# A one-core decoder layer: memory tokens fetched together ahead of the first step of dilated values, and the values' stores issued from the ACT queue

## The chip, the cores and the metric

The kernel runs on one core of a Trainium2 chip. The metric is the device time of one execution in microseconds (us); the time of a kernel is the median of several runs. The core has five engines that each work through their own list of instructions in order: TensorE (PE in the profile) multiplies matrices and transposes, VectorE (DVE) and ScalarE (ACT) do elementwise work, GpSimd (POOL) a little of it, and SyncE (SP) does nothing here but issue transfers (DMAs) between device memory and on-chip memory. Instructions of different engines are ordered only by semaphores: an instruction that waits holds everything behind it on its own engine.

## The reference

One layer on 512 tokens of width 1024, all in float32. Around every part stand a norm before and a norm after, with a gain each:

```
h = x + 0.5 * post(SwiGLU_1(pre(x)))
u = pre(h)
proj = u @ w_in                      # recurrence q,f,i,gate | dilated q,k,v x3 | memory queries | branch gates
y_hg  = gated linear recurrence (HGRN2) on chunks of 64 tokens, 4 heads of 128
y_dil = sliding-window attention at dilations 1, 4, 16, merged over the three
y_mem = softmax(mq @ mk.T) @ mv,   mk, mv = split(rmsnorm(mem, mem_norm_w) @ w_mem_kv)
y = sum over branches of sigmoid(gate_b) * (y_b @ w_br_b)
h = h + post(y @ w_out)
h = h + 0.5 * post(SwiGLU_2(pre(h)))
```

`mem` holds 256 memory tokens of width 1024. They are normed, transposed and projected to keys and values; this does not depend on the 512 tokens.

## The kernel before

Matrices are kept with the contracted index on the 128 partitions. Every float32 operand of a big product is split into two parts: a rounded one, hi, that ACT writes, and the rest, lo, that DVE writes (`split`, L160). A product is three matmuls (hi·hi, hi·lo, lo·hi), L333 to L335 for 512 columns and L353 to L355 for 256. Pairs of weight columns go through a scheme of seven half-size products in place of eight (`pair`, L358); their sums of weights are made by DVE (`total`) or by an adding transfer that POOL issues (L302).

The mixing part (`mixing`, L900) runs a list of steps, `ORDER` (L42). Those that matter here: "hg0" and "hg1" project two heads of the recurrence each (three `pair` calls: f, q and the output gate), "v1", "v2" and "v0" project the values of one dilation for all four heads, "prep" norms and transposes the memory tokens, and "kv" projects them.

- A values step (`values`, L837) loads a 1024x512 block of weights in four pieces of 512 KB, splits it, and makes four blocks of 24 matmuls, one for each 128 tokens. ACT copies each block out of PSUM (L850), and `put_values` (L853) stores it to device memory, from where the attention later reads it in another order of rows.
- The step "prep" starts `mem_prep` (L523), a Python generator. For each of two tiles of 128 tokens it fetches two halves of 256 KB (L530), squares them on ACT (L174, the sum of squares comes along), raises the sum to the power -1/2 on POOL (L181), scales by it and the gain on DVE (L190) and transposes on PE, two groups of four (L344). ACT and DVE split what the transposes give into the tiles `mT`.

The order of all work comes from a small planner in Python. Each matmul that is written advances a clock (`tick`, L109). A generator that yields a number of microseconds is picked up again that much later (`LAT`, L47), and what it then writes lands between the matmuls of the main steps. So the engines' lists are fixed in advance; a matmul or transpose whose operand is late holds the PE list behind it. All fetches are issued on SP. Those made by `fetch` (L139) stand in the SP list in the order written; weight loads (`bring`, L145) may move up but keep their mutual order. A transfer on SP waits for its target's buffer to be free, and also for the transfer eight places earlier in the rotation of eight completion semaphores. Buffers: 4 stages of 512 KB for weights, 18 split weights, 37 slots of 128x512, 5 weight sums, and 3 PSUM banks (`px`) for all side work.

Names in the lists of instructions: `st`, `sh` are staged weights, `sum` a weight sum, `w` a split weight, `s` a slot, `v` the values in device memory, `ps` and `px` PSUM banks of the main steps and of side work, `ident` the identity matrix of a transpose.

Of the kernel before, what the change touches and what calls it, by code (L numbers as in the profile page):

```python
# [17 lines left out]
P = 128  # L18
# [20 lines left out]
NST = 4  # L39
HT = T // 2  # L40

ORDER = ("hg0", "v1", "prep", "hg1", "v2", "kv", "v0", "dil0", "mq0", "mq1", "dil1", "b_hg", "b_mem", "b_dil")  # L42

CHUNKS1 = (2, 4, 4, 4, 4, 4)
CHUNKS2 = (2, 4, 4, 4, 4, 4)

LAT = dict(comb=1.0, mem0=0.5, mem1=8.0, mem2=1.5, hg=1.5, hgx=6.0, hg1=6.0, hg2=11.0, hg3=6.0, hg4=6.0, dil0=4.0, dil1=17.0, dil2=5.0,  # L47
           dil3=3.0, norm=8.0, mnorm=5.0, start=0.1, step=2.0, keep=2.0)
PLAN = dict(early1=2, plain1=2, early2=2, plain2=2)
HALVES = (slice(0, 512), slice(512, 1024))  # L50


class Layer:
# [469 lines left out]
    def mem_prep(self, mem, w, mT):  # L523

        gain = self.bcast_gain(w)
        for t in range(2):
            ts = slice(t * P, (t + 1) * P)
            m = [self.slot() for _ in range(2)]
            for hf in range(2):
                self.fetch(m[hf], mem[ts, HALVES[hf]])  # L530
            hf = 0
            for x in self.normed(m, gain, LAT['mnorm'], self.paux):
                if isinstance(x, float):
                    yield x
                    continue
                for i in range(2):
                    hi, lo = mT[2 * hf + i]
                    self.split(hi[:, :, ts], lo[:, :, ts], x[:, 2 * i:2 * i + 2, :])
                hf += 1
# [313 lines left out]
    def put_values(self, v, name):  # L853

        d = self.dram.tile([T, 512], F32, tag=name, name=name)
        for t in range(NT):
            self.nc.sync.dma_start(out=d[t * P:(t + 1) * P, :], in_=v[t][:, 0, :])
        return d

    def get_values(self, d, g, hp):  # L860
# [39 lines left out]
    def mixing(self, a, ready, nbias):  # L900
# [41 lines left out]
        z, vd = None, {}  # L942
        for n, step in enumerate(ORDER):
            if step in ("hg0", "hg1"):
# [18 lines left out]
            else:  # L963
                b, y, tasks, w = {"b_hg": (0, y_hg, t_hg, "w_br_hg"), "b_mem": (2, y_mem, t_mem, "w_br_mem"), "b_dil": (1, y_dil, t_dil, "w_br_dil")}[step]
                self.need(*tasks)
                z = self.branch(b, y, w_in, a[w][0], z, n == len(ORDER) - 1)
        return z
# [140 lines left out]
```

## Time and profile before

| what | value |
| --- | --- |
| time, median of 3 runs | 1394.15 us (1392.47 to 1395.41) |
| the profiled execution's own time | 1396.16 us |
| its span in the trace | 1394.4 us |
| mean granted clock of TensorE | 0.988 of full speed |
| busy: PE, DVE, ACT, POOL | 1341.6, 1016.6, 744.5, 161.8 us (96, 73, 53, 12% of the span) |
| DMA: share of the 16 engines on SP's queue, on POOL's | 41.6%, 16.4% |

The profile lists one execution. PE is busy in nearly all of it, so what counts is where PE stands still, which instruction it stood before, and whether its clock was lowered after it. The clock column gives the granted clock as a share of 2.4 GHz: 1.00 is full speed and 0.50 is 1.2 GHz. Busy times of the other engines are averages over stages; only in the stretch around a PE wait do they say something about the time.

The steps of interest in the trace: "v1" runs its 96 matmuls from 428 to 450.6 us, "hg1" follows until 504 us, then "v2".

### The profile page before, as it was taken

What the parts mean: (1) busy time and instruction counts of PE and PEld (TensorE: products, weight loads), DVE (VectorE), ACT (ScalarE), POOL (GpSimd) and SP (SyncE); (2) the same over time, 40 slices, a digit from 0 to 9 for tenths busy, and PEclk for the clock granted to TensorE, in tenths of its full rate; (3) what the DMA queues carried; (4) which work ended last, traced back from release to release, by engine and by line L of the source; (5) the groups of instructions that cost most, each with busy time, mean ns of one, the idle gap of its engine ahead of it and who ended that gap; (6) DMA issues with size and microseconds to landing.
All of it is one profiled execution on the core that took longest, in us unless ns stands there. A gap on an engine that the chain in (4) does not pass through costs nothing.

```text
span 1394.4 us, 24579 instructions
## 1 busy us (share of the span) xinstructions
PE 1341.6 (96%) x9197; PEld 1242.3 (89%) x9197; DVE 1016.6 (73%) x1932; ACT 744.5 (53%) x1527; POOL 161.8 (12%) x204
## 2 busy tenths in 40 slices
PE   6999999999999699998899999999999999999997
PEld 6999999999788688898889899999889999999995
DVE  6887777776888574576777787787569777767765
ACT  6675545554576464353655555555457655445541
POOL 1011110110200100111201201110010100100000
PEclk9999999999999899999899999999999999999998
DMA  9676565656536534576456656665365776655513
GB/s 269 141 185 180 137 151 148 158 143 179 175 96 178 150 106 136 148 184 150 103 126 149 166 127 160 154 163 131 111 219 145 175 181 160 150 145 140 149 46 136
DMA packets 264238, 210.95 MB, mean 151 GB/s; under 512 B 10645, under 2 KB 216886, under 8 KB 264118
## 3 DMA queue, kind: packets, MB, share of 16 engines
q1 hardware_dynamic: 242870, 171.56, 41.6%
q0 software_dynamic: 21248, 37.82, 16.4%
q8 instruction: 72, 1.18, 0.4%
q14 instruction: 48, 0.39, 0.1%
HBM read 162.12 MB, written 9.47 MB: 123 GB/s over the span
## 4 chain that ended last, share of the span: by engine, by line
PE 46%; DVE 3%; issue 2%; DMA 2%; ACT 0%; POOL 0%; DVEq 0%; POOLq 0%; ACTq 0%
PE ps L354 9%; PE ps L355 9%; PE ps L353 9%; PE ps L334 3%; PE ps L333 3%; PE ps L335 3%; PE px L340 2%; PE px L333 2%; PE px L334 2%; PE px L335 2%; DVE s L158 1%; DVE w L158 1%; PE px L344 1%; DMA sh<-in_w_in_dram 1%; DMA sum<-sh 1%
## 5 line engine op out<-in xcount | busy, mean ns | idle before, releaser
L161 ACT ACTIVATE w<-sum 128x512 fp32r<-128x512 f32 x288 | 180.1, 631 | 222.1 <-PE ps L354 174.9
L158 DVE TENSOR_TENSOR w<-sum,w 128x512 fp32r<-128x512 f32 x288 | 196.6, 689 | 87.1 <-ACT w L161 85.5
L353 PE MATMUL ps<-xhi,w 128*128 128x256 f32 x864 | 247.4, 286 | 0.9 <-ACT s L371 0.9
L355 PE MATMUL ps<-xhi,w 128*128 128x256 f32 x864 | 246.0, 285 | 0.7 <-DVE w L158 0.7
L354 PE MATMUL ps<-xlo,w 128*128 128x256 f32 x864 | 245.5, 284 | 0.0
L161 ACT ACTIVATE w<-st 128x512 fp32r<-128x512 f32 x260 | 163.5, 630 | 137.4 <-PE ps L354 97.1
L158 DVE TENSOR_TENSOR w<-st,w 128x512 fp32r<-128x512 f32 x260 | 177.3, 689 | 34.0 <-ACT w L161 32.1
L158 DVE TENSOR_TENSOR s<-s,s 128x256 f32<-128x256 f32 (+3 forms) x316 | 177.2, 566 | 19.0 <-ACT s L161 4.2
L353 PEld LDWEIGHTS ps<-xhi,w 128*128 128x128 f32 x864 | 166.7, 193 | 3.5 <-ACT s L371 1.1
L354 PEld LDWEIGHTS ps<-xlo,w 128*128 128x128 f32 x864 | 166.5, 193 | 2.5 <-issue 0.2
L355 PEld LDWEIGHTS ps<-xhi,w 128*128 128x128 f32 x864 | 166.8, 193 | 0.9 <-DVE w L158 0.9
L302 POOL DMA_DIRECT2D sum<-st x72 | 62.7, 871 | 642.9 <-DVE s L158 374.9
L158 DVE TENSOR_TENSOR sum<-sum,st 128x512 f32<-128x512 f32 x144 | 99.3, 690 | 46.0 <-issue 34.9
L158 DVE TENSOR_TENSOR s<-s,ps 128x256 f32<-128x256 f32 (+1 forms) x194 | 92.5, 478 | 33.5 <-PE ps L335 25.0
L333 PE MATMUL px<-s,s 128*128 128x512 f32 x288 | 112.6, 391 | 0.0
L334 PE MATMUL px<-s,s 128*128 128x512 f32 x288 | 112.5, 391 | 0.0
L335 PE MATMUL px<-s,s 128*128 128x512 f32 x288 | 112.0, 389 | 0.0
L302 POOL DMA_DIRECT2D sum<-sh x72 | 63.6, 883 | 301.2 <-DMA sh<-in_w_in_dram 101.5
L353 PE MATMUL ps<-t3hi,w 128*128 128x256 f32 x288 | 83.3, 289 | 0.5 <-DVE s L158 0.5
L353 PE MATMUL ps<-t4hi,w 128*128 128x256 f32 x288 | 82.0, 285 | 0.8 <-ACT s L374 0.8
L354 PE MATMUL ps<-t3lo,w 128*128 128x256 f32 x288 | 82.5, 286 | 0.0
L353 PE MATMUL ps<-t2hi,w 128*128 128x256 f32 x288 | 82.4, 286 | 0.0
(185 smaller groups left out, 3433.4 us busy)
## 6 DMA issues: line engine op xcount, KB each, us to landing
st<-in_ffn_w_gu_dram SPq DMA_DIRECT2D x48, 512.0 KB, 4.8
st<-in_w_in_dram SPq DMA_DIRECT2D x48, 512.0 KB, 4.2
st<-in_ffn_w_down_dram SPq DMA_DIRECT2D x44, 512.0 KB, 3.9
sum<-in_ffn_w_gu_dram SPq DMA_DIRECT2D x80, 256.0 KB, 3.3
sum<-sh POOLq DMA_DIRECT2D x72, 256.0 KB, 3.8
sum<-st POOLq DMA_DIRECT2D x72, 256.0 KB, 3.8
sum<-in_w_in_dram SPq DMA_DIRECT2D x64, 256.0 KB, 3.2
sh<-in_ffn_w_gu_dram SPq DMA_DIRECT2D x40, 256.0 KB, 3.5
```

What stands on the lines that cost most here:

```text
L158: self.pin(self.nc.vector.tensor_tensor(out=out, in0=a, in1=b, op=op))
L161: self.pin(self.nc.scalar.activation(hi, src, AF.Copy))
L302: self.nc.gpsimd.dma_start(out=u, in_=x, accum_op=ALU.add)
L333: mm(out, lhsT=lhs[0], rhs=rhs[0], start=first, stop=False)
L334: mm(out, lhsT=lhs[0], rhs=rhs[1], start=False, stop=False)
L335: mm(out, lhsT=lhs[1], rhs=rhs[0], start=False, stop=last)
L340: self.nc.tensor.matmul(out, lhsT=lhsT, rhs=rhs, start=start, stop=stop, **k)
L344: self.nc.tensor.transpose(out, in_, self.ident)
L353: mm(out, lhsT=lh, rhs=rh, start=first and k == 0, stop=False, skip_group_check=True)
L354: mm(out, lhsT=lh, rhs=rl, start=False, stop=False, skip_group_check=True)
L355: mm(out, lhsT=ll, rhs=rh, start=False, stop=k == 3, skip_group_check=True)
```

## The change

Three edits. The list of steps has "prep" ahead of "v1" and no longer behind it. `mem_prep` fetches both tiles of memory tokens (four halves) at once, directly behind the two halves of the gain, and then yields a new latency `mload` of 10 us before the first norm; before, it fetched a tile when its turn came. And `put_values` issues its stores from the ACT queue (`nc.scalar`) where it was SP's (`nc.sync`).

```diff
-ORDER = ("hg0", "v1", "prep", "hg1", "v2", "kv", "v0", "dil0", "mq0", "mq1", "dil1", "b_hg", "b_mem", "b_dil")
+ORDER = ("hg0", "prep", "v1", "hg1", "v2", "kv", "v0", "dil0", "mq0", "mq1", "dil1", "b_hg", "b_mem", "b_dil")
...
-           dil3=3.0, norm=8.0, mnorm=5.0, start=0.1, step=2.0, keep=2.0)
+           dil3=3.0, norm=8.0, mnorm=5.0, mload=10.0, start=0.1, step=2.0, keep=2.0)
...
         gain = self.bcast_gain(w)
+        ms = [[self.slot() for _ in range(2)] for _ in range(2)]
+        for t in range(2):
+            for hf in range(2):
+                self.fetch(ms[t][hf], mem[t * P:(t + 1) * P, HALVES[hf]])
+        yield LAT['mload']
         for t in range(2):
             ts = slice(t * P, (t + 1) * P)
-            m = [self.slot() for _ in range(2)]
-            for hf in range(2):
-                self.fetch(m[hf], mem[ts, HALVES[hf]])
             hf = 0
-            for x in self.normed(m, gain, LAT['mnorm'], self.paux):
+            for x in self.normed(ms[t], gain, LAT['mnorm'], self.paux):
...
-            self.nc.sync.dma_start(out=d[t * P:(t + 1) * P, :], in_=v[t][:, 0, :])
+            self.nc.scalar.dma_start(out=d[t * P:(t + 1) * P, :], in_=v[t][:, 0, :])
```

What this makes of the engines' lists, first on SP, before, from the last weight piece that is loaded during "v1" on (`st_6030`; `v_5451` are the values of "v1", `s_5464` a half of the gain, `s_5468` and `s_5613` halves of the two tiles of memory tokens):

```order
L151 DMA st_6030<-in_w_in_dram 128x2x512
L857 DMA v_5451<-s_5332 128x512
...
L151 DMA sum_5730<-in_w_in_dram 128x4x128
...
L151 DMA st_6040<-in_w_in_dram 128x2x512
L857 DMA v_5451<-s_5449 128x512
L141 DMA s_5464<-in_mem_norm_w_dram 128x512
...
L141 DMA s_5468<-in_mem_dram 128x512
...
L151 DMA sh_5728<-in_w_in_dram 128x4x128
L151 DMA st_6050<-in_w_in_dram 128x2x512
L151 DMA sh_6816<-in_w_in_dram 128x4x128
L151 DMA sum_6818<-in_w_in_dram 128x4x128
L141 DMA s_5613<-in_mem_dram 128x512
```

And now, from the same weight piece on (it is called `st_6051`):

```order
L151 DMA st_6051<-in_w_in_dram 128x2x512
L141 DMA s_5265<-in_mem_norm_w_dram 128x512
L141 DMA s_5266<-in_mem_norm_w_dram 128x512
L141 DMA s_5269<-in_mem_dram 128x512
L141 DMA s_5270<-in_mem_dram 128x512
L141 DMA s_5271<-in_mem_dram 128x512
L141 DMA s_5272<-in_mem_dram 128x512
L151 DMA sum_5730<-in_w_in_dram 128x4x128
L151 DMA sum_5733<-in_w_in_dram 128x4x128
L151 DMA st_6061<-in_w_in_dram 128x2x512
L151 DMA sh_5728<-in_w_in_dram 128x4x128
```

The six loads have moved ahead of the next weight sums, the four stores of "v1" have left the list, and no weight load stands between the two tiles of memory tokens.

On PE, before, the transposes of the first tile (`px_5595`, `px_5604`) stand in "hg1", behind the first product of its second pair (`ps_5736`):

```order
L335 MATMUL ps_5420<-w_5293,xlo_91 128x512
L353 MATMUL ps_5506<-xhi_88,w_5509 128x256
...
L340 MATMUL px_5582<-s_5364,s_5360 128x128 x4
L344 MATMUL px_5588<-ident,s_5361 128x128 x4
...
L355 MATMUL ps_5736<-xhi_88,w_5740 128x256
L344 MATMUL px_5595<-ident,s_5482 128x128 x4
...
L344 MATMUL px_5604<-ident,s_5484 128x128 x4
```

Now they stand in "v1", ahead of its fourth block (`ps_5486`), and those of the second tile (`px_5512`, `px_5521`) in the third product of the first pair of "hg1":

```order
L335 MATMUL ps_5411<-w_5313,xlo_91 128x512
L344 MATMUL px_5452<-ident,s_5405 128x128 x4
L344 MATMUL px_5461<-ident,s_5407 128x128 x4
L333 MATMUL ps_5486<-w_5279,xhi_88 128x512
...
L354 MATMUL ps_5617<-t1lo,w_5618 128x256
L344 MATMUL px_5512<-ident,s_5480 128x128 x4
L355 MATMUL ps_5617<-t1hi,w_5619 128x256
L353 MATMUL ps_5617<-t1hi,w_5618 128x256
L344 MATMUL px_5521<-ident,s_5482 128x128 x4
L340 MATMUL px_5603<-s_5384,s_5380 128x128 x4
```

Between the two groups for the second tile and the end of "v1" there are 12 + 12 + 8 matmuls of 256 columns. Four matmuls of the recurrence of "hg0" (L340) come right behind.

On DVE, before, the elementwise work of the recurrence of "hg0" (the last four of it here) is followed at once by the lo parts of the weights of "hg1":

```order
L158 TENSOR_TENSOR s_5388<-s_5388,s_5111 128x512
L158 TENSOR_TENSOR s_5389<-s_5389,s_5111 128x512
L158 TENSOR_TENSOR s_5384<-s_5384,s_5321 128x512
L158 TENSOR_TENSOR s_5385<-s_5385,s_5321 128x512
L158 TENSOR_TENSOR w_5532<-sum_5528,w_5531 128x512
L158 TENSOR_TENSOR w_5550<-sum_5490,w_5549 128x512
```

Now the scaling of the first tile (`v_5401` and the two L190) stands amid it:

```order
L158 TENSOR_TENSOR s_5381<-s_5381,s_5328 128x512
L180 TENSOR_SCALAR v_5401<-ss_1119_5395,ss_1121_5398 128x1
L190 SCALAR_TENSOR_TENSOR s_5405<-s_5269,r_5402,s_5265 128x512
L190 SCALAR_TENSOR_TENSOR s_5407<-s_5270,r_5402,s_5266 128x512
L158 TENSOR_TENSOR s_5418<-s_5369 128x512
...
L158 TENSOR_TENSOR s_5419<-s_5419,s_5341 128x512
L158 TENSOR_TENSOR s_5258<-px_5452,s_5257 128x2x128
L158 TENSOR_TENSOR w_5586<-sum_5582,w_5585 128x512
...
L180 TENSOR_SCALAR v_5476<-ss_1136_5470,ss_1138_5473 128x1
L158 TENSOR_TENSOR w_5705<-sh_5542,w_5704 128x512
L190 SCALAR_TENSOR_TENSOR s_5480<-s_5271,r_5477,s_5265 128x512
```

Six instructions of the recurrence now come behind the scaling of the first tile, and then, up to that of the second, eight weight instructions of 512 columns and four lo parts of the transposed tokens of 256.

## Rows read from the trace of the kernel before

**Rows 1.** Waits of PE, whole span: what waited for whom, total us, times, longest.

```profile
PE px L344 <- DVE s L190: 22.4, 8, 9.1
```

**Rows 2.** Timeline of PE around v1 and hg1, and one row near 1036: start, us, instruction, idle before.

```profile
445.17 0.39 PE L333 MATMUL ps<-w,xhi 128*128 128x512 f32 x1
...
450.61 0.28 PE L353 MATMUL ps<-xhi,w 128*128 128x256 f32 x1
...
452.04 0.28 PE L353 MATMUL ps<-t2hi,w 128*128 128x256 f32 x1
...
466.02 1.09 PE L344 MATMUL px<-ident,s 128*128 128x128 f32 x4 [6.74 <-DVE s L190]
...
478.44 0.63 PE L344 MATMUL px<-ident,s 128*128 128x128 f32 x4 [3.06 <-DVE s L190]
481.07 1.09 PE L344 MATMUL px<-ident,s 128*128 128x128 f32 x4 [2.00 <-DVE s L158]
...
1035.85 0.38 PE L334 MATMUL ps<-xlo,w 128*128 128x256 f32 x1 [1.94 <-DVE xlo L158]
```

**Rows 3.** Windows: length, busy PE, PEld, DVE, ACT, POOL, clock, DMA, GB/s.

```profile
466.00:468.90 2.90, 2.88 (x14) 2.90 (x15) 2.90 (x7) 0.38 (x1) 0.00 (x0) 0.51 0.17 30
...
481.00:486.00 5.00, 4.93 (x24) 4.96 (x25) 3.32 (x10) 3.11 (x6) 0.00 (x0) 0.51 0.00 0
...
435.00:438.00 3.00, 3.00 (x15) 2.49 (x14) 1.99 (x6) 2.97 (x5) 0.00 (x0) 1.00 1.13 306
438.00:441.00 3.00, 3.00 (x15) 2.49 (x14) 3.00 (x4) 2.60 (x6) 0.00 (x0) 1.00 0.33 126
440.00:455.00 15.00, 15.00 (x85) 13.17 (x84) 14.48 (x24) 11.71 (x24) 0.65 (x1) 1.00 0.36 116
560.00:580.00 20.00, 20.00 (x107) 16.59 (x106) 7.41 (x15) 3.66 (x7) 1.78 (x2) 1.00 0.58 156
1033.00:1036.00 3.00, 1.06 (x6) 0.67 (x5) 2.56 (x5) 2.34 (x7) 0.75 (x1) 1.00 0.61 232
```

**Rows 4.** Timeline of SP's queue, 432 to 500 us: start, us, transfers issued.

```profile
433.67 0.37 SPq L151 DMA_DIRECT2D st<-in_w_in_dram  x1
438.81 8.85 SPq L857 DMA_DIRECT2D v<-s  x3
...
454.01 0.93 SPq L141 DMA_DIRECT2D s<-in_mem_dram  x2
...
469.79 2.65 SPq L141 DMA_DIRECT2D s<-in_mem_dram  x2
```

**Rows 5.** Waits of SP's queue, whole span.

```profile
SPq L857 <- ACT s L850: 52.9, 11, 8.7
```

**Rows 6.** Timeline of ACT, 432 to 500 us.

```profile
442.43 0.62 ACT L640 ACTIVATE s<-s 128x512 f32<-128x512 f32 x1
...
460.63 0.63 ACT L174 ACTIVATE s<-s 128x512 f32<-128x512 f32 x1 [4.94 <-DMA s<-in_mem_dram]
...
461.92 0.63 ACT L174 ACTIVATE s<-s 128x512 f32<-128x512 f32 x1 [0.57 <-DMA s<-in_mem_dram]
...
475.90 0.61 ACT L174 ACTIVATE s<-s 128x512 f32<-128x512 f32 x1
```

**Rows 7.** Timeline of DVE, 445 to 495 us.

```profile
445.32 2.50 DVE L158 TENSOR_TENSOR s<-s,s 128x512 f32<-128x512 f32 x4
...
470.65 0.76 DVE L158 TENSOR_TENSOR s<-px,s 128x256 fp32r<-128x256 f32 x2 [1.29 <-ACT s L161]
...
477.54 1.42 DVE L190 SCALAR_TENSOR_TENSOR s<-s,r,s 128x512 f32<-128x512 f32 x2 [0.69 <-POOL r L181]
```

**Rows 8.** DMA issues of the page: KB each, median us from issue to landing.

```profile
v<-s SPq DMA_DIRECT2D x12, 256.0 KB, 2.0
```

## Prediction, on record before the changed kernel ran

> **What bounds the kernel now.** I read four views, in this order: the page's busy times with the clock, the waits of PE, the timeline of PE where these waits lie, and the timelines of SP, ACT and DVE in the same stretch. PE is the bound: it is busy nearly throughout, so a change can gain only where PE stands still or runs at a lowered clock. The waits of PE show one large entry, transposes (L344) that wait for the scaled tile from DVE's L190 [rows 1]. The rest of that entry lies at the start of the kernel and at the other norms, which the change does not touch. In the timeline the reader is to see three stops of PE inside "hg1", each in front of a transpose: 6.74, 3.06 and 2.00 us, in all 11.8 us [rows 2]. They are the transposes of the memory tokens. After the stops the granted clock is 0.51, so PE runs at 1.2 instead of 2.4 GHz: 2.88 us of work in 466.0 to 468.9 and 4.93 us in 481.0 to 486.0 [rows 3]. This is 7.81 us of work that would take half as long, so another 3.9 us. Together the memory tokens cost 11.8 + 3.9 = 15.7 us.
>
> Why the tokens are late stands in the timeline of SP. After the weight load at 433.67 the queue holds the stores of the values, and each of these waits on SP for ACT's copy: the three stores begin at 438.81 and take 8.85 us until all are issued [rows 4]. Over the whole span SP waited 52.9 us for such copies [rows 5]. The first tile of tokens is issued only at 454.01, and ACT's squares wait for it until 460.63 and 461.92 [rows 4, 6]. The second tile stands behind a weight load whose buffer is still in use and goes out at 469.79.
>
> **The loads, earlier.** In the new SP list the six loads come right behind the weight load of 433.67. That is issued by 434.04; a pair takes 0.93 us [rows 4], so the gain goes out until 434.97, the first tile until 435.90, the second until 436.83. Their targets have been free long before by the order of the list. From issue to use the two halves of the first tile took 460.63 - 454.01 = 6.6 and, issued half a pair later, 461.92 - 454.48 = 7.4 us [rows 4, 6]. Taken over, the halves are there at 441.6 and 442.9. This is an estimate with two ends: it can be sooner, which gains nothing (next paragraph), and it can be later, since the DMA engines are full until about 439 (share 1.13, then 0.33 [rows 3]) and the loads add 6 x 256 KB = 1.5 MB. At the 306 GB/s of that row this takes 4.9 us, so everything has landed by 444, and by 445 with one us for completion. I take the measured 7.4 us.
>
> **First stop that is left (S1).** PE reaches the first transposes behind three blocks of "v1", at 445.17, where the fourth block starts now [rows 2]. ACT gets to the squares behind the exponentials of "hg0", whose last one before that point starts at 442.43 and takes 0.62 us [rows 6]; with one store issued by ACT itself, for which I take SP's 0.37 us for a load [rows 4], that is 443.4. The second square starts some 0.6 us later, at 444.0. From the start of the second square to the transpose it took 478.44 - 475.90 = 2.54 us [rows 2, 6], through DVE, POOL and DVE again. So PE goes on at 446.5: S1 = 1.4 us. Bounds: with no issue cost 1.0; with the second half landing at 445 it is 445 + 2.54 - 445.17 = 2.4; with the landing 1.5 us later still, 4.
>
> **Second stop that is left (S2).** The tile's scaling stands in DVE's list amid the recurrence of "hg0", and DVE is busy 14.48 of 15 us there [rows 3], so what comes behind is pushed back. The scaling starts 0.9 us ahead of the transpose (477.54 against 478.44 [rows 2, 7]), at 445.6, and its two instructions take 1.42 us: 447.1. Then come six instructions of the recurrence at 2.50 / 4 = 0.63 us, 3.8 us; eight weight instructions, 5.0 us; four lo parts at 0.76 / 2 = 0.38 us, 1.5 us [rows 7]. That is 457.4. POOL's power, whose operand is made one instruction before the end of this list, adds about 0.3 us, and the scaling again 0.9 us to the transpose: 458.6. PE gets there by 446.5 + 0.9 (two groups of transposes) + 5.44 (a block, 445.17 to 450.61) + 32 matmuls at 1.43 / 12 = 0.12 us, 3.8 us [rows 2], at 456.7. So S2 = 1.9 us. Bounds: 0, if DVE gains 2 us by finding its operands ready, and 4, if ACT's splits, which alternate with DVE's here, come late by as much.
>
> **Clock.** A stop of 1.94 us near 1036 left the granted clock at 1.00 [rows 2, 3]; the stop of 3.06 us was followed by the lower clock. S1 and S2 lie nearer to the first. I take no loss, and 3.9 / 2 = 2 us for each stop as the other end.
>
> **What lies beside other work.** The stores no longer hold up SP, but the loads behind them feed splits that PE did not wait for here, so this alone gains nothing. On ACT the twelve stores cost at most 12 x 0.37 = 4.4 us; eight of them lie in "v2" and "v0", where ACT is as little busy as 3.66 of 20 us and PE fully [rows 3]. A store waits there only for ACT's own copy and for a transfer issued long before. The four of "v1" have their price in S1 and S2. With PE 12 us earlier, the weights of the next pairs are wanted earlier: counting on through both lists with the same durations, DVE has the first summed weight of the second pair of "hg1" at about 465, and PE wants it at about 469 (estimates).
>
> The Trainium skill speaks against the second part of the change. "DMA: Bandwidth & Descriptors", section "Issuing engines are not separate DMA queues", says that transfers issued by different engines run on the same 16 DMA engines and interleave, and that issuing from several engines saves only the sequencer's time. By it the first store of "v1", no longer behind the loads but beside them, can put off the tokens by its 256 KB, 0.9 us at 306 GB/s, S1 would be 2.3 and the time 0.9 us longer. The rows agree in that the engines are full just there (1.13 [rows 3]); they do not show two queues side by side at this place, and the store is issued only near 439, when the loads are mostly under way.
>
> **Sum.** 15.7 - 1.4 - 1.9 = 12.4 us less. The profiled execution took 1396.16 us (span 1394.4), so its counterpart would take 1383.8 us (span 1382.0). The median of the runs is 1394.15, 2.0 us below the profiled one; the prediction for the median is 1394.15 - 12.4 = 1381.8 us. Runs of this kernel differ by some 3 us, so I call 0.2% (2.8 us) the least that can be told from no change.
>
> **Rivals.**
> - Both stops vanish, because DVE keeps up: the whole 15.7 us, 1378.5. For it: PE is the bound elsewhere at the same mix of work. Against it: ACT is not free for the squares before 443.
> - The tokens stay late: the DMA engines are full when the loads are issued, S1 and S2 become 4 us each and each is followed by the lower clock, 2 us each. That is 12 of 15.7 us, so 1390.4. For it: the DMA share of 1.13; against it: only 1.5 MB stand in front or beside.
> - DVE becomes the bound. The scaling and lo parts of two tiles, 2 x (1.42 + 4 x 0.38 + 0.2) = 6.3 us, used to fall into PE's stops and are now added where DVE has 0.5 us free in 15. If PE has to wait for all of them beyond S1 and S2, 15.7 - 3.3 - 6.3 = 6.1 us are left: 1388.
> - Slower: ACT is held by its own stores. If an issue on ACT blocks it until the transfer has landed, the first two stores of "v1", one ahead of the squares and one ahead of the weight splits, put off everything behind them. The median landing is 2.0 us [rows 8], under load up to 7.4 as above: 2 x 7.4 = 14.8 us on the path, the lower clock twice 4 us, S1 and S2 3.3 us, against 15.7 us: 1394.15 + 6.4 = 1400.5. It decides from (15.7 - 3.3 - 4) / 2 = 4.2 us a store. Against it: on SP three stores and their waits went out in 8.85 us, and the next load followed, so an issue does not hold its queue until landing.
> - The change does not do what it says: the loads stay behind something on SP (a buffer, or one of the eight semaphores). The transposes then wait as before, 1394. Against it: the transfers that the loads wait for by rotation all stand ahead of the weight load of 433.67 in the list.
>
> **How the numbers follow.** Chances: the forecast 0.52, both stops gone 0.12, late tokens 0.15, DVE bound 0.12, slower by ACT 0.05, no effect 0.04. The forecast's own range is S1 + S2 from 1 to 5.7, so 1379.5 to 1384.2. The range of 8 in 10 takes in both stops gone and reaches over the DVE case to late tokens: 1378 to 1390.5. Faster by over 0.2%: 0.52 + 0.12 + 0.12 + 0.12 of the late tokens = 0.88. Within 0.2%: 0.04 and 0.03 of the late tokens, 0.07. Slower: 0.05.
>
> **What would show it.** In the profile after: SP issues the tokens at about 435 to 437, not 454 and 470. PE has a stop of 1 to 2.4 us before the first transposes near 445 and one of about 2 us near 457, none of 6.74 us, and "v2" begins some 12 us earlier. The clock stays at 1.00 from 440 to 500. Wrong would be: squares that still wait for the tokens beyond 445, the clock at 0.5 in "v1" or "hg1", stops of PE in front of weights (L353 to L355) after 460, or idle time of ACT right behind its stores.

## The result, and the profile after

The kernel after takes 1377.81 us (median of 4 runs, 1376.86 to 1380.12), the kernel before 1394.78 us beside it: a ratio of 0.9879, 95% interval 0.9858 to 0.9900, which is 17.0 us less. Predicted were 1381.8 us and a range from 1378.0 to 1390.5. So the direction and the place were right, and the fall was larger than the whole range allowed, by 0.2 us. The profiled execution of after has a span of 1375.1 us.

PE's waits, its stops in v1 and hg1, and the clock (length, busy PE, PEld, DVE, ACT, POOL, clock, DMA, GB/s) in the profile after; they answer to [rows 1 to 3]:

```profile
PE px L344 <- DVE s L190: 15.9, 7, 10.4
```

```profile
445.76 1.29 PE L344 MATMUL px<-ident,s 128*128 128x128 f32 x8 [1.22 <-DVE s L190]
...
457.80 0.63 PE L344 MATMUL px<-ident,s 128*128 128x128 f32 x4 [1.44 <-DVE s L190]
```

```profile
440.00:500.00 60.00, 57.31 (x418) 51.96 (x417) 48.65 (x97) 39.71 (x83) 7.13 (x9) 1.00 0.54 151
```

Three stops of together 11.8 us have become two, S1 = 1.22 and S2 = 1.44 us, and the clock is at full speed (2.4 GHz) in all of these 60 us, where before two stretches ran at half. SP's queue and ACT's timeline in the same place [rows 4 and 6], and the scalings on DVE [rows 7]:

```profile
434.98 2.00 SPq L141 DMA_DIRECT2D s<-in_mem_dram  x4
...
452.60 1.33 SPq L151 DMA_DIRECT2D sum<-in_w_in_dram  x2
```

```profile
435.53 1.28 ACT L623 ACT_TABLE_LOAD   x1
436.18 0.35 ACTq L859 DMA_DIRECT2D v<-s  x1
...
442.61 0.62 ACT L174 ACTIVATE s<-s 128x512 f32<-128x512 f32 x1
...
443.23 0.62 ACT L174 ACTIVATE s<-s 128x512 f32<-128x512 f32 x1
```

```profile
444.87 1.41 DVE L190 SCALAR_TENSOR_TENSOR s<-s,r,s 128x512 f32<-128x512 f32 x2 [0.68 <-POOL r L181]
...
456.90 1.41 DVE L190 SCALAR_TENSOR_TENSOR s<-s,r,s 128x512 f32<-128x512 f32 x2 [0.44 <-POOL r L181]
```

All four halves of the tokens are issued by 437 us. The squares have no wait in brackets: the tokens were there. The issue of a store at 436.18 lies inside the table load of 435.53 to 436.81, so ACT lost nothing by it. Behind the next store, of 444.43, ACT stands still for 2.5 us, but what it waits for there is an operand from DVE, whose list now has the scaling ahead of it. The page's line for these stores, against [rows 8]:

```profile
v<-s ACTq DMA_DIRECT2D x12, 256.0 KB, 2.6
```

Behind hg1, however, PE kept gaining. Since executions start up to 3 us apart, the table compares stretches, worked out from PE's timeline: "v1 to v0" runs from the first matmul of L333 in v1 to the first of L353 behind v0, "dil0 to dil1" from there to the next L333 behind dil1. The last column goes from the stop of some 5 us at the start of the memory queries (664 us before, 651 after) to the next one (683 and 668 us). The experiments below are in it. The rows between which the stretches of the first profiles lie, first before, then after, each with the recurrence's matmuls that stand near the end of "hg1":

```profile
427.96 0.40 PE L333 MATMUL ps<-w,xhi 128*128 128x512 f32 x1
...
504.08 0.40 PE L333 MATMUL ps<-w,xhi 128*128 128x512 f32 x1
...
505.22 1.06 PE L340 MATMUL px<-s,s 128*128 128x128 f32 x8
...
588.85 0.28 PE L353 MATMUL ps<-xhi,w 128*128 128x256 f32 x1
...
797.47 0.40 PE L333 MATMUL ps<-s,w 128*128 128x512 f32 x1
```

```profile
428.00 0.40 PE L333 MATMUL ps<-w,xhi 128*128 128x512 f32 x1
...
490.89 1.06 PE L340 MATMUL px<-s,s 128*128 128x128 f32 x8
...
492.58 0.40 PE L333 MATMUL ps<-w,xhi 128*128 128x512 f32 x1
...
575.55 0.28 PE L353 MATMUL ps<-xhi,w 128*128 128x256 f32 x1
...
778.56 0.40 PE L333 MATMUL ps<-s,w 128*128 128x512 f32 x1
```

| profile | v1 to v0 | of it v1, hg1 | dil0 to dil1 | between stops |
| --- | --- | --- | --- | --- |
| before, three profiles | 160.9, 161.0, 160.8 | 76.1, 76.2, 76.0 | 208.6, 208.9, 204.7 | 19.1, 18.7, 18.8 |
| stores on ACT only, two | 162.7, 160.9 | 78.0, 76.1 | 201.3, 207.1 | 17.8, 19.1 |
| loads early only, two | 149.0, 148.3 | 66.0, 65.4 | 205.3, 204.9 | 17.9, 17.7 |
| after, two | 147.6, 147.8 | 64.6, 64.9 | 203.0, 203.6 | 17.7, 17.9 |
| step moved only | 158.6 | 75.6 | 203.3 | 17.3 |
| joint loads, old place, two | 150.8, 151.6 | 66.0, 66.8 | 199.7, 203.1 | 17.5, 18.6 |
| transposes later | 149.5 | 66.5 | 205.6 | 18.2 |
| norms together | 151.9 | 68.8 | 202.2 | 17.9 |
| merge later: before, after | 161.6, 148.8 | 76.8, 65.8 | 205.2, 205.6 | 18.5, 17.9 |

In "v1 to v0" two profiles of one kernel differ by 0.2 to 0.8 us, but for one of 162.7, and after stands 13.2 us below before. The column "of it v1, hg1" shows only 11.4 us, since eight matmuls and eight transposes of the recurrence that before come behind "hg1" (the first rows above have the matmuls at 505.22) now stand in it (490.89), so "v1 to v0" is the stretch to compare. In "dil0 to dil1" profiles of one kernel differ by up to 6 us. Ahead of v1 and behind dil1 the five profiles of before and after agree within 3.0 and 1.3 us, in no order by kernel.

### The profile page after: what moved, and what is told of

The parts are those of the page before. It is cut to its first block, busy times and chain, and to the rows that moved or that the text cites. A ratio compares the mean times of both kernels' runs of the same rounds, so it can differ in the third digit from the quotient of the medians.

```text
span 1375.1 us, 24568 instructions
## 1 busy us (share of the span) xinstructions
PE 1333.8 (97%) x9197; PEld 1236.2 (90%) x9197; DVE 1015.6 (74%) x1932; ACT 742.5 (54%) x1527; POOL 161.9 (12%) x204
## 4 chain that ended last, share of the span: by engine, by line
PE 43%; DVE 4%; DMA 3%; issue 2%; ACT 1%; POOL 1%; SPq 0%; DVEq 0%; POOLq 0%; ACTq 0%
PE ps L353 8%; PE ps L355 8%; PE ps L354 8%; PE ps L334 3%; PE ps L333 3%; PE ps L335 3%; PE px L334 2%; PE px L333 2%; PE px L335 2%; PE px L340 2%; DVE s L158 1%; DVE w L158 1%; DMA sh<-in_w_in_dram 1%; PE px L344 1%; DMA sum<-sh 1%
## 5 line engine op out<-in xcount | busy, mean ns | idle before, releaser
L353 PE MATMUL ps<-xhi,w 128*128 128x256 f32 x864 | 247.1, 286 | 1.9 <-ACT s L371 1.9
L353 PEld LDWEIGHTS ps<-xhi,w 128*128 128x128 f32 x864 | 166.2, 192 | 4.8 <-ACT s L371 2.1
L333 PE MATMUL px<-s,s 128*128 128x512 f32 x288 | 112.6, 391 | 0.0
L353 PE MATMUL ps<-t3hi,w 128*128 128x256 f32 x288 | 82.6, 287 | 0.7 <-DVE s L158 0.7
L353 PE MATMUL ps<-t4hi,w 128*128 128x256 f32 x288 | 82.2, 285 | 0.0
L353 PE MATMUL ps<-t2hi,w 128*128 128x256 f32 x288 | 81.9, 284 | 0.0
```

The lines of the kernel that those rows point to most:

```text
L333: mm(out, lhsT=lhs[0], rhs=rhs[0], start=first, stop=False)
L353: mm(out, lhsT=lh, rhs=rh, start=first and k == 0, stop=False, skip_group_check=True)
```

## The experiments

What the expectations call the stretch from the start of v0 is the table's "dil0 to dil1": it starts where v0 ends.

**The two halves of the change, each alone.** The loads early, the stores back on SP:

```diff
-            self.nc.scalar.dma_start(out=d[t * P:(t + 1) * P, :], in_=v[t][:, 0, :])
+            self.nc.sync.dma_start(out=d[t * P:(t + 1) * P, :], in_=v[t][:, 0, :])
```

> The kernel after, but with the stores of the values back on SP. Where the change gained is split in two: 12 us in v1 and hg1 (428 to 504 us), and 5 to 7 us that PE gained later, at the memory queries and the second dilation step (650 to 800 us), which the prediction did not have. Theory A (all comes from the early loads; the later part is a matter of when PE arrives there, or of single executions): 1377.8 us as after, within 1.5, and the loads of the tokens still go out near 435 to 437 us. Theory B (the later part comes from SP, which the stores no longer hold up in v2 and v0): 1383 to 1385 us, with the half clock back near 655 to 690 us. Theory C (the stores held up the weight loads behind them in v1 too): over 1386 us, with stops of PE in front of weights in hg1.

Measured: 1377.64 us (6 runs, 1375.38 to 1383.45), ratio to before 0.9890 (0.9865 to 0.9916), as fast as after. Its SP queue:

```profile
435.42 1.99 SPq L141 DMA_DIRECT2D s<-in_mem_dram  x4
437.50 7.67 SPq L859 DMA_DIRECT2D v<-s  x2
453.03 1.33 SPq L151 DMA_DIRECT2D sum<-in_w_in_dram  x2
```

The stores hold the queue for 7.67 us again, but now behind the tokens; the weight sums behind them go out at 453.03 against 452.60 in after, where no store stands in front of them, so something else holds them in both. Theory A holds in time. A second profile of the same kernel took 204.9 us in "dil0 to dil1", just under the 205 that theory B asked for, at a time that is that of after (1378.33):

> The kernel with the early joint fetch and the stores back on SP, for a second profile. From the start of v0 to the end of dil1 the three profiles with the stores on SP took 208.6, 208.9 and 205.3 us, and the three with the stores on ACT 201.3, 203.0 and 203.6. Theory B (the stores on SP cost 3 to 5 us there): 205 us or more again. Theory A (single executions differ by that much): as likely below 204 as above.

The other half, the kernel before with the opposite edit:

> The kernel before with one edit: the stores of the values issued from ACT. Order of the steps and the fetches stay. On SP the gain and the first tile stood behind the fourth store (452.65 us); now they stand behind a weight load whose stage comes free at about 451, so the first tile goes out some 1.5 us earlier, and the second still waits for its buffer near 469. Theory A (the early loads are all of the gain): 1393 us, 1391.5 to 1394.8; PE still stops some 5 us and 5 us in front of the memory transposes in hg1. Theory B (SP freed from the stores gives the later 5 to 7 us): 1386 to 1388 us, the half clock near 665 to 690 us gone, the stops in hg1 as before.

Measured: 1390.82 us (12 runs), ratio 0.9975 (0.9955 to 0.9995), some 3.5 us less than before by the ratio, with bounds of 0.7 and 6.3, so neither theory's time is met (A: 1391.5 or more, B: 1388 or less). Its SP queue and PE:

```profile
451.43 1.35 SPq L141 DMA_DIRECT2D s<-in_mem_dram  x2
...
468.38 2.43 SPq L141 DMA_DIRECT2D s<-in_mem_dram  x2
```

```profile
464.60 1.09 PE L344 MATMUL px<-ident,s 128*128 128x128 f32 x4 [6.39 <-DVE s L190]
...
478.37 1.09 PE L344 MATMUL px<-ident,s 128*128 128x128 f32 x4 [3.04 <-DVE s L190]
481.45 1.09 PE L344 MATMUL px<-ident,s 128*128 128x128 f32 x4 [2.00 <-DVE s L158]
```

The tokens go out 2.6 and 1.4 us earlier (0.9 of it because v1 itself starts earlier in this execution), and the three stops stay, as theory A said. The 201.3 us behind v0 spoke for theory B; a second profile took that back (207.1 us, 1393.39 us in all):

> The kernel before with the stores on ACT alone, second profile. From the start of v0 to the end of dil1 the first took 201.3 us, 7 us less than before. If the freed SP queue gives that: 200 to 203 again. If it was a lucky execution: 204 to 208.

**Is the later gain of the kernel or of one execution?** Both kernels once more, unchanged:

> The kernel before once more, for a second profile: does the granted clock fall at the same three later places (after the stops at 664, 683 and 790 us)? If the later 5 to 7 us are of this kernel and not of one execution, the stops of 4.9, 2.2 and 2.1 us and the half clock behind each are there again within 0.3 us. If they are chance, at least one of the three differs: a stop of under 1.5 us or a clock of 1.00 behind it.

> The kernel after once more, for a second profile. If the later gain is of this kernel: stops of about 4.7, 1.1 and 2.1 us near 651, 668 and 772 us, with the clock at half only behind the first. If it is chance: a half clock behind the second or the third in this profile.

> The kernel before, third profile. From the third later stop (2.12 us near 790) to the end of dil1 the two profiles of before took 7.6 and 7.7 us at a lowered clock, and between the first and the second later stop 19.1 and 18.7 us; with either half of the change these are 6.1 and 17.3 to 17.9 us. If that belongs to the kernel before: 7.6 and 18.7 to 19.1 again. If it is chance: 6.1 or 17.8 in one of them.

They took 1393.88, 1375.53 and 1389.69 us. The stops recur in the second profile of before (5.03, 2.56, 2.12 us), the clock behind them does not: it was lowered behind the second stop in the first profile and at 1.00 in the second, and in the third, with a stop of 3.06 us, it was lowered there and not behind the third stop. The windows behind the second stop, first profile, then second:

```profile
683.45:690.45 7.00, 7.00 (x42) 6.70 (x43) 6.47 (x27) 4.33 (x17) 0.00 (x0) 0.76 0.25 44
```

```profile
683.00:690.00 7.00, 7.00 (x56) 6.90 (x57) 7.00 (x32) 5.35 (x20) 0.00 (x0) 1.00 0.24 42
```

So this part of the loss comes and goes. After's second profile has stops of 4.75, 1.16 and 2.12 us, with the lowered clock behind the first alone, as was expected if the later gain is of the kernel. What does recur is the last column: 18.7 to 19.1 us in before, 17.3 to 18.2 in nine of ten profiles of kernels that issue the tokens together or before v1. One profile with late tokens has the short time too, the first with the stores on ACT only (17.8 us). DVE waits for the exchange of the statistics (`ot`), ahead of the maxima of the memory queries in its list; first before's second profile, then after's (before's three have waits of 1.48 to 1.52 us, and that first profile with the stores on ACT only has 0.73):

```profile
679.82 0.17 DVE L158 TENSOR_TENSOR mm<-st,ot 128x4 f32<-128x4 f32 x1 [1.50 <-DMA ot<-x]
```

```profile
661.82 0.16 DVE L158 TENSOR_TENSOR mm<-st,ot 128x4 f32<-128x4 f32 x1 [0.71 <-DMA ot<-x]
```

**What of the early loads counts.** First the step moved ahead of v1, without the joint fetch and the latency:

```diff
-        ms = [[self.slot() for _ in range(2)] for _ in range(2)]
-        for t in range(2):
-            for hf in range(2):
-                self.fetch(ms[t][hf], mem[t * P:(t + 1) * P, HALVES[hf]])
-        yield LAT['mload']
...
+            m = [self.slot() for _ in range(2)]
+            for hf in range(2):
+                self.fetch(m[hf], mem[ts, HALVES[hf]])
...
-            for x in self.normed(ms[t], gain, LAT['mnorm'], self.paux):
+            for x in self.normed(m, gain, LAT['mnorm'], self.paux):
```

> The step prep ahead of v1 and the stores on ACT, as in the kernel after, but each tile fetched when its turn comes and no latency of 10 us ahead of the first norm. The first transposes then stand some 38 matmuls into v1, which PE reaches near 437 us. Theory A (what counts is that the transposes are written late enough for the loads): the tokens are issued at 435 to 436 and land at 441.6 to 443, so the scaled tile is there near 445.4 and PE stops some 8.8 us, with 3 us more of half clock behind it; S1 and S2 go: 1377.8 - 2.7 + 8.8 + 3 = 1387 us, 1385 to 1391. Rival (moving the step ahead of v1 is the gain, the latency only a detail): 1377 to 1380 us, with stops of 1 to 3 us in v1.

Measured: 1389.32 us (10 runs), ratio 0.9977 (0.9961 to 0.9993). Its PE, and the window behind the stop:

```profile
441.55 1.94 PE L344 MATMUL px<-ident,s 128*128 128x128 f32 x8 [7.45 <-DVE s L190]
```

```profile
441.50:450.00 8.50, 8.45 (x30) 7.11 (x31) 3.93 (x10) 4.96 (x11) 0.55 (x1) 0.67 0.01 2
```

```profile
465.83 0.39 PE L355 MATMUL ps<-t2hi,w 128*128 128x256 f32 x1 [2.56 <-DVE w L158]
```

All loads went out by 434.5 us, and still PE stood 7.45 us, followed by 8.5 us at a mean clock of 0.67 (8.45 x 0.33 = 2.8 us lost): theory A. A loss that neither theory had comes behind it: 2.56 us in front of a weight, whose lo part DVE makes only at 465.10, behind the recurrence's work. An earlier load with its use right behind it gains little: 2.3 us in "v1 to v0". Then the reverse, the joint fetch and the latency with the step behind v1:

```diff
-ORDER = ("hg0", "prep", "v1", "hg1", "v2", "kv", "v0", "dil0", "mq0", "mq1", "dil1", "b_hg", "b_mem", "b_dil")
+ORDER = ("hg0", "v1", "prep", "hg1", "v2", "kv", "v0", "dil0", "mq0", "mq1", "dil1", "b_hg", "b_mem", "b_dil")
```

> The kernel after with the step prep back behind v1; the joint fetch, the latency of 10 us and the stores on ACT stay. The six loads stand behind the weight load of 451 us and go out at about 452 to 454.7, the first transposes stand far into hg1, which PE reaches near 464 us without a stop. Theory A (what counts is the joint fetch and a latency that covers it, not the place ahead of v1): tokens there at 460 to 462, scaled by 464, stops of together 0 to 2 us: 1375 to 1379 us. Rival (the place ahead of v1 is needed, since behind it weight loads hold the queue): stops of 4 us or more in hg1 with half clock behind them, 1383 to 1390 us.

Measured: 1377.37 us (6 runs), ratio 0.9902 (0.9877 to 0.9927); a second profile took 1381.16 us:

> The joint fetch with the step behind v1, second profile. The first took 66.0 us in v1 and hg1 (1.5 more than after, with one stop of 4.9 us) and 199.7 us from v0 to the end of dil1, so that the whole was as fast as after. If both belong to the kernel: 66 and 199 to 201. If the second is chance: 66 and 202 to 205, and a time of 1379 to 1382.

The 199.7 us were chance, as the second part of that expectation has it. SP, PE and DVE of the first profile:

```profile
449.44 2.56 SPq L141 DMA_DIRECT2D s<-in_mem_dram  x4
```

```profile
472.43 1.12 PE L344 MATMUL px<-ident,s 128*128 128x128 f32 x4 [4.90 <-DVE s L687]
```

```profile
463.65 1.41 DVE L190 SCALAR_TENSOR_TENSOR s<-s,r,s 128x512 f32<-128x512 f32 x2 [2.15 <-POOL r L181]
...
472.03 0.34 DVE L687 SCALAR_TENSOR_TENSOR s<-s,dec,px 128x128 f32<-128x128 f32 x1
```

The scaled tile is there at 465.1, 7 us before the transpose: tokens issued at 449 are early enough. The stop that is left, of 4.90 us, ends with the recurrence (L687), which reads a PSUM bank of side work, and not with the tokens. With the lowered clock behind it (a mean of 0.79 from 472 to 480 us) it looks like what the rival said, but it has another cause, and the time is theory A's. So most of the gain, 10.1 and 9.3 of 13.2 us in "v1 to v0", needs the joint fetch with its latency, not the place ahead of v1.

**Can S1 and S2 go?** Later transposes, by the planner alone:

```diff
-           dil3=3.0, norm=8.0, mnorm=5.0, mload=10.0, start=0.1, step=2.0, keep=2.0)
+           dil3=3.0, norm=8.0, mnorm=8.0, mload=12.0, start=0.1, step=2.0, keep=2.0)
```

> The kernel after with the planner's latencies mload 12 and mnorm 8 in place of 10 and 5, so both groups of transposes stand some 4 us of PE work later; all fetches and stores stay. If S1 and S2 (1.22 and 1.44 us) are only a matter of where the transposes stand, both go: 1377.8 - 2.7 = 1375.1 us, 1373.5 to 1376.5, and v1 with hg1 takes 62 us in place of 64.6. Rival (DVE is the bound in this stretch, the scaling gets as much later as the transposes): stops of 1 us or more stay, in front of transposes or of weights, and the time is 1377.8 within 1.5.

Measured: 1378.32 us (6 runs), ratio 0.9892 (0.9868 to 0.9917), no change against after: the rival. PE and DVE:

```profile
447.52 1.03 PE L344 MATMUL px<-ident,s 128*128 128x128 f32 x8
...
458.66 0.63 PE L344 MATMUL px<-ident,s 128*128 128x128 f32 x4 [3.03 <-DVE s L190]
```

```profile
457.76 1.42 DVE L190 SCALAR_TENSOR_TENSOR s<-s,r,s 128x512 f32<-128x512 f32 x2 [0.85 <-POOL r L181]
```

S1 is gone, S2 has doubled, and behind it the clock was lowered (a mean of 0.79 from 458 to 466 us): v1 starts at 425.51 here and at 428.00 in after, so the second scaling starts 32.3 us into v1 and no longer 28.9. It stands behind more of DVE's list. So both norms were written together, ahead of that:

```diff
+        norms = [self.normed(ms[t], gain, LAT['mnorm'], self.paux) for t in range(2)]
+        lats = [next(n) for n in norms]
         for t in range(2):
...
-            for x in self.normed(ms[t], gain, LAT['mnorm'], self.paux):
-                if isinstance(x, float):
-                    yield x
-                    continue
+            yield lats[t]
+            for x in norms[t]:
```

with mnorm at 7.

> The kernel after with the norms of both tiles written together behind the latency of 10 us (four squares, two powers, four scalings), then the transposes of the first tile 7 us and of the second 14 us later by the planner. So the scalings stand early in DVE's list and both groups of transposes later than now. If S1 and S2 are work of DVE and ACT that stands too late in their lists: no stop in front of either group, v1 with hg1 62 us in place of 64.6, 1375 us (1373.5 to 1376.5). Rival (DVE is full from 440 to 459 us, so whatever is put ahead holds back the weights or the recurrence): the stops come back elsewhere in hg1, in front of weights or of the recurrence's products, 2 us or more together, and the time is 1377.5 within 1.5.

Measured: 1381.94 us (6 runs), ratio 0.9924 (0.9896 to 0.9952). PE, and DVE at the new stop:

```profile
446.29 1.03 PE L344 MATMUL px<-ident,s 128*128 128x128 f32 x8
...
454.85 1.03 PE L344 MATMUL px<-ident,s 128*128 128x128 f32 x8
...
473.70 0.39 PE L353 MATMUL ps<-t3hi,w 128*128 128x256 f32 x1 [2.91 <-DVE s L158]
```

```profile
472.36 0.69 DVE L158 TENSOR_TENSOR sum<-sum,st 128x512 f32<-128x512 f32 x1 [4.18 <-DMA sum<-sh]
```

Neither group of transposes waits, and the stop is back 19 us later, behind an adding transfer of weights that DVE waited 4.18 us for. The clock behind it was lowered (a mean of 0.76 from 473 to 480 us). The rival is right that the stop comes back, and half right on the cause: what comes late is a weight sum, through POOL's transfer, not through DVE's own work. The time is neither theory's: 1381.94 lies 2.9 us above the rival's upper end, and "v1 to v0" is 4.2 us longer than in after. Why that transfer was late was not tried.

**The exchange of the statistics.** `dil1` raised from 17 to 21 in both kernels, so that the merge that waits for the exchange should stand behind the memory queries' maxima:

> The kernel before with the latency dil1 at 21 in place of 17: the merge of the statistics (DVE's maximum over own and exchanged values) stands later in DVE's list, so DVE no longer waits for the exchange ahead of the scores of the memory queries, and PE not for their exponentials. Theory E (that stop of 2.2 to 3.1 us and the half clock behind it are what the kernel before loses beyond the tokens): 1390 us, 3 to 4 us less than before, with less than 1 us in front of these scores. Theory F (the rest is spread of executions): the stop goes but the time is 1392 to 1394.

> The kernel after with the same edit, dil1 at 21. Its stop at this place was 1.12 and 1.16 us without half clock behind it. Theory E: 1 us less than after, 1376.8, so that the two kernels with the edit are 13 to 14 us apart. Theory F: 1376.8 as well, but 16 to 17 us apart.

Measured: before with the edit 1394.42 us (12 runs), ratio 1.0010 (0.9993 to 1.0028); after with it 1379.55 us (6 runs), ratio 0.9915 (0.9891 to 0.9939). DVE and PE of the first:

```profile
678.35 0.16 DVE L158 TENSOR_TENSOR mm<-st,ot 128x4 f32<-128x4 f32 x1 [1.08 <-DMA ot<-x]
```

```profile
681.29 1.13 PE L340 MATMUL px<-s,s 128*128 128x256 f32 x4 [2.27 <-ACT s L575]
```

The wait and the stop are still there, so the edit did not do what it was written for. The time of before with it is not theory E's (1390); the two kernels are 14.9 us apart in their medians and 13.2 by their ratios, which is nearer to E than to F. Since both theories took the stop to be gone, this one settles nothing.

## Why the prediction failed, and what it had right

The place and the mechanism there were right; the forecast time was 4.0 us too high (1381.8 said, 1377.81 measured), and the measured one lies below the whole range. The step that failed is "What lies beside other work": it priced the later work of "hg1" and put all that stands behind "hg1" at nothing. In the profiles "dil0 to dil1" took 208.6, 208.9 and 204.7 us before (mean 207.4) and 203.0 and 203.6 after (mean 203.3). Two smaller parts are the size of S1 and S2 and the base from which the sum was taken off.

- **The loads, earlier.** Right: issued at 434.98 to 436.98 (said: 434.97 to 436.83). That it fits so closely is in part luck: the weight load ahead was out 0.8 us sooner than said, and the gain's two halves took 1.65 us and not 0.93. The squares start at 442.61 and 443.23 and wait for no token (said: tokens there at 441.6 and 442.9).
- **S1.** Said 1.4, measured 1.22 us. From the second square to the transpose it took 445.76 - 443.23 = 2.53 us, as taken over (2.54). The square was 0.8 us earlier than said: 0.37 us since the store's issue cost ACT nothing beside the table load, the rest since the exponentials ahead of it were done earlier. PE was 0.6 us earlier as well.
- **S2.** Said 1.9, measured 1.44 us. Counting through DVE's list gave the transpose at 458.6, measured 457.80, with PE there at 456.36 (said 456.7). From the first scaling to the second it took 456.90 - 444.87 = 12.0 us (said 12.1). The mechanism is DVE's list, as the later transposes showed.
- **Clock.** Right in v1 and hg1: 1.00 from 440 to 500 us, behind S1 and S2 too. The row that the prediction took for the stop near 1036 ends 0.15 us behind that stop; the 9 us after it ran at 1.00 as well, so the reading holds.
- **The stores on ACT.** Right that they do not hold ACT, so the rival with ACT held until landing falls: the store of 436.18 was issued inside other work, though landing took 2.6 us in the median. With the loads early it makes no difference which engine issues them (1377.64 us on SP, 1377.81 on ACT). The prediction had the first store of "v1" out only near 439, when the loads are mostly under way; it went out at 436.18, beside them. The Trainium skill's rule that was weighed ("DMA: Bandwidth & Descriptors", section "Issuing engines are not separate DMA queues") would have put 0.9 us on S1; S1 shows none, since nothing waited for the tokens. That section of the Trainium skill also says that the issuing engine saves little but the issue itself, which agrees with these two times.
- **The sum.** Before v0 it was nearly right: in "v1 to v0" it said 12.4 us; the profiles give 160.9 - 147.7 = 13.2, of which 0.64 is S1 and S2 (3.3 said, 2.66 measured). Its price of 15.7 us for the old stops and their clock held (13.2 + 2.66 = 15.9). Of the 4.0 us this difference is 0.8. Another 0.8 is the base: the median of three runs was 1394.15, that of all 67 runs of before in these comparisons is 1393.4 (1386.85 to 1398.86). The remaining 2.4 us are left for what stands behind v0.
- **What of this is shown.** The 13.2 us are: each of the two kernels repeats its stretch within 0.3 us, and the experiments tie it to the loads and the place of their use. The later part is shown in part. About 1 us of it lies between the two stops at the memory queries, together with a longer wait for the exchange of the statistics; it is there in all three profiles of before and in neither of after, but one other profile with late tokens lacks it, and one with the joint fetch has it (18.6 us). Pooled, the six profiles with late tokens have a mean of 206.0 us in "dil0 to dil1" (201.3 to 208.9) and the ten others 203.6 (199.7 to 205.6). The difference is the size of the 2.4 us, and the two ranges overlap. So a later gain of the kernel is likely, not shown, and its cause stays open.
- **Theory B**, that the stores' leaving SP gives the later part, is not borne out by the profiles: 201.3 and 207.1 us in two of the same kernel. The 12 runs with only the stores moved still lie 0.7 to 6.3 us below before, where the prediction said that this alone gains nothing, and "v1 to v0" shows no gain there; that too stays open.
- **The range.** Its low end was set at both stops gone, as if the place of the change were the only one that could move. It should have carried the spread of the other stretches: the prediction took some 3 us from three runs, and single runs of before lie 12 us apart.
- **The rivals.** The time lies nearest to "both stops vanish" (1378.5), yet the stops are there: a time alone would have confirmed the wrong mechanism. "DVE becomes the bound" fell for after, but DVE's list is what kept S2 when the transposes were moved; each of the two attempts on S1 and S2 got a stop of some 3 us back. The rival with ACT held has a slip: 1400.5 counts 4 us for the lower clock in all, not "twice 4 us".

No version tried beats after beyond its interval.

## What to carry to other kernels

An early load gains only with the use put late enough behind it: the same loads cost 7.45 us of stop with the use right behind them, and in the kernel after, with 10 us of the planner's time between, no square waited for them. A use that is moved later gains only as far as its producer does not move with it; read the producer's place in its own engine's list first. And where runs of one kernel spread by 0.4% to either side, compare stretch by stretch over two or three profiles: one stretch repeats within 0.8 us in all kernels but one and carries the argument, another varies by up to 6 us and carries none from a single pair of profiles.

## What the runs showed that was not expected

The clock behind a short stop is not settled by the stop's length. Behind the third later stop, of 2.12 us in both, the second profile of before ran at a mean of 0.76 and the second of after at 1.00 (PE, then the window; first before, then after):

```profile
787.66 1.84 PE L340 MATMUL px<-s,s 128*128 128x128 f32 x8 [2.12 <-DVE s L158]
```

```profile
788.00:795.00 7.00, 7.00 (x49) 7.00 (x48) 4.42 (x9) 4.84 (x15) 2.43 (x3) 0.76 0.75 159
```

```profile
770.35 1.13 PE L340 MATMUL px<-s,s 128*128 128x128 f32 x8 [2.12 <-DVE s L158]
```

```profile
770.00:780.00 10.00, 9.65 (x74) 9.38 (x75) 5.83 (x18) 8.00 (x25) 4.60 (x7) 1.00 0.59 131
```

7.00 x 0.24 is 1.7 us from the same instruction behind the same stop. Other runs stretch this further. In the second profile with the loads early only, a stop of 1.65 us, with one of 0.50 us a little later, was followed by a mean of 0.73 (762.63 to 769 us); in the second with the stores on ACT only, one of 2.93 us was followed by 1.00 (680.5 to 688 us):

```profile
762.63 0.39 PE L353 MATMUL ps<-t3hi,w 128*128 128x256 f32 x1 [1.65 <-DVE s L158]
```

```profile
680.78 0.70 PE L340 MATMUL px<-s,s 128*128 128x256 f32 x2 [2.93 <-ACT s L575]
```

So in this kernel a stop of some 2 us should be priced at itself plus nothing or plus 1.5 to 2 us, and not at one of the two.
